# Forming half of w_out's operands beside the first stage, moving the second gate's vector into the feed-forward, and setting the gates' steps later

## The chip, the cores and the metric

The kernel runs on one core of a Trainium2 chip, written in Bass with tile pools: the engines are TensorE (PE), VectorE (DVE), ScalarE (ACT), GpSimd (POOL) and SyncE (SP), which issues nearly all DMAs. Each engine works through its own instructions in order and waits on semaphores for the others. The metric is the device time of one execution in microseconds (us), the median of several runs. A profile is of one further execution.

## The reference

One layer of a hybrid encoder on a sequence of 2048 rows and 1024 columns, in f32: a modulated norm, one input projection that feeds both banded attention (8 heads, 2 key heads) and a bidirectional mLSTM (4 heads, chunks of 128), an output projection, then a SwiGLU feed-forward, and a last norm.

```python
def hybrid_layer(x, c, w_mod, b_mod, ...):
    mod = jax.nn.silu(c) @ w_mod + b_mod
    shift1, scale1, gate1, shift2, scale2, gate2 = split(mod, 6)
    hmix = rms_norm(x, g_norm1) * (1.0 + scale1) + shift1
    proj = hmix @ w_in
    q_a, k_a, v_a, q_m, k_m, v_m, o_m, gates = split(proj, IN_SPLITS)
    att = rms_norm(banded_attention(q_a, k_a, v_a, sink), g_attn_out)
    q_m, k_m = split(silu(centred_dwconv(concat([q_m, k_m]), conv_w, conv_b)), 2)
    i_f, f_f, i_b, f_b = split(gates + b_gates, 4)
    h_m = sigmoid(o_m) * rms_norm(mlstm(fwd) + mlstm(bwd), g_mlstm_out)
    x = x + gate1 * (concat([att, h_m]) @ w_out)
    hff = rms_norm(x, g_norm2) * (1.0 + scale2) + shift2
    gte, up = split(hff @ w_ffn_in, 2)
    return x + gate2 * ((silu(gte) * up) @ w_ffn_out)
```

Two parts matter here: the six vectors of `mod` (rows 0 to 5 of a 1024 x 6144 product; row 2 is gate1, rows 3 and 4 are the feed-forward's shift and scale, row 5 is gate2), and `gate1 * (... @ w_out)`, where the kernel multiplies gate1 into w_out's columns ahead of the product.

## The kernel before

A product in f32 is made of three fast matmuls: each operand is split into a high and a low part (`whi`, `wlo`; ScalarE copies the high part in the fast type, VectorE or GpSimd subtracts), and high x high, high x low and low x high are added in PSUM. TensorE does nearly nothing else, and its order is written out by hand; the other engines' order follows from where the code puts their steps between TensorE's.

**First stage, to about 181 us.** The rows of x are normed, turned and split, and 16 tiles of 128 rows (`tt` 0 to 15) go through the natural projections: `nat_mm` (48 matmuls to a tile, into `pa` and `pv`) gives the values of both attentions, stored in `vst_d` and `vaug_d`, and the gates' pre-activations `gn`. Between the tiles `mod_row(m)` (L359 to L395) forms the vectors of the modulation that are needed later, in two halves of 512 columns: four loads of `wmod`, eight multiply-adds on VectorE into `macc`, a split into `macch` and `maccl`, and a pair of matmuls with ones (`modrow`, L381 and L382). For rows 3 and 4, ScalarE then copies the result to `mrow` (L388), and VectorE turns it into columns (L391). For rows 2 and 5, the gates, VectorE adds the bias (`brow`) and it is stored in `gate_d`. `vecs` gives a half a tile from tile 8 on; before that, row 2 is formed.

**The conv's weights.** `proj_cols` and `cols_steps` (L241 on) load 128 columns of w_in into `wraw`, which has one buffer; `whi` is copied by ScalarE (L251), and four pieces of `wlo` are subtracted by GpSimd (L254). The first such weight, `w_first`, is formed ahead of tile 12; the next, called the second weight below, is loaded when the window begins.

**The window, from 181 to about 245 us.** TensorE runs conv tiles (`gps` L498; 24 matmuls each, eight values of k by three products). Every single matmul is a pull: the generators `gates()` and `w_out_ops()` are given the count of pulls, and go on when it has reached the number that they yielded. Where `gates()` yields 36, its next matmuls (`rps` L871) are issued behind the 36th pull. The gates' chain goes: transposes of `gn`; two copies on ScalarE (L842, L843); exp and log, scans and row sums on VectorE (L845 to L867); `rps`; eight scans `mn` (L881) and the row steps up to `rw` (L888); `cps` (L892); the exponentials; the last transposes. A conv tile writes into one of the `gps` banks of PSUM; ScalarE's copy `cacc` (L525) and VectorE's two side steps (L512, L513) empty it. `w_out_ops()` multiplies w_out's rows by gate1 (`gb`) and forms sums and differences (`ts`) for the products' operands, all on GpSimd, and stores them in `wo_d`. It has eight items: two halves of the columns (`c_`) by four blocks of rows (`k`).

**Later stages.** mLSTM heads 0 to 3 to 573 us, each with a loop backward over the chunks (`cc` from 15 to 0) and one forward; `prep` forms the mask `ng` of a chunk (GpSimd L629, then ScalarE L635) for the forward loop. Attention to 790, the out-projection to 1000, the feed-forward's first product (`fp`) in pairs to 2005, its second (`fo`) to the end. `norm2` forms the feed-forward's input in steps between the pairs.

Of the kernel before, what the change touches and what calls it, by code (L numbers as in the profile page):

```python
# [11 lines left out]
F32 = mybir.dt.float32  # L12
# [24 lines left out]
def hybrid_layer_kernel(  # L37
# [106 lines left out]

    xs, s2s = ExitStack(), ExitStack()
    hp = ctx.enter_context(tc.tile_pool(name="big", bufs=1, side="left"))
# [131 lines left out]
    with tc.tile_pool(name="sw", bufs=2, side="right", reuse_waits="tile") as sw:  # L278
# [80 lines left out]
        def mod_row(m):  # L359

            for z in range(2):
                acc = sw.tile([P, 512], F32, tag="macc", name="macc", bufs=1)
                if m in (2, 5):
                    br = (s1 if m == 2 else wp).tile([1, 512], F32, tag="mrow" if m == 2 else "oth", name="brow", bufs=1)
                    sp.dma_start(br, b_mod[:, m * D + z * 512:m * D + (z + 1) * 512])
                for k in range(0, KT, 2):
                    w = (hp if "b" in wrow[0] else sw if "m" in wrow[0] else wp).tile([P, 2, 512], F32, tag=wrow[0], name="wmod", bufs=1)
                    wrow.rotate(-1)
                    sp.dma_start(w, w_mod[k * P:(k + 2) * P, m * D + z * 512:m * D + (z + 1) * 512]
                                 .rearrange("(k p) c -> p k c", p=P))  # L370
                    for i in range(2):
                        if k + i == 0:
                            dve.tensor_scalar(acc, w[:, 0, :], sc_col[:, 0:1], None, MUL)
                        else:
                            dve.scalar_tensor_tensor(acc, w[:, i, :], sc_col[:, k + i:k + i + 1], acc, MUL, ADD)
# [5 lines left out]
                pe.matmul(ps, ones_r, hi, start=True, stop=False)  # L381
                pe.matmul(ps, ones_r, lo, start=False, stop=True)  # L382
                if m in (2, 5):
                    dve.tensor_tensor(br, ps[:1, :], br, ADD)
                    sp.dma_start(gate_d[m // 5:m // 5 + 1, z * 512:(z + 1) * 512], br)
                    continue
                row = sw.tile([P, 512], F32, tag="macch", name="mrow", bufs=1)
                act.activation(row, ps, AF.Copy)  # L388
                for k in range(4):
                    rk = row[:, k * P:(k + 1) * P]  # L390
                    dve.tensor_tensor_reduce(out=rk, in0=rk, in1=ident, op0=MUL, op1=ADD, scale=1.0, scalar=0.0,  # L391
                                             accum_out=mod[:, m, 4 * z + k:4 * z + k + 1])
            if m not in (2, 5):
                o = O_BM + m * KT
                dve.tensor_tensor(mod[:, m, :], mod[:, m, :], cols[:, o:o + KT], ADD)  # L395

        def nat_mm(n, i, pa, pv, ks):
# [46 lines left out]
        for n in range(NB):  # L444
# [5 lines left out]
            if n == 1:  # L450
# [4 lines left out]
                dve.tensor_scalar(gml, cols[:, O_GM:O_GM + HM], 0.5, None, MUL)  # L455
            if n + 1 == NB:
                w_first = proj_cols(C_KM)
            for i in range(4):
                tt = 4 * n + i
                if tt < 3:  # L460
                    pa, pv = ops[i]
                else:
                    pa, pv = bank("g", "pa"), bank("a", "pv")
# [4 lines left out]
                if tt == 8:  # L468
# [126 lines left out]
    def mlstm(h, nb, nf, last):  # L595
# [45 lines left out]
        for cc in list(range(NT - 1, 0, -1)) + [0, 0, 0]:  # L641
# [6 lines left out]
            if cc in (6, 4, 2):  # L648
                bcs[3 - cc // 2] = load_bc(3 - cc // 2)
            if cc:  # L650
                todo.append((cc, *k_chunk(blk[n][0][:, i * P:(i + 1) * P], blk[n][1][:, i, :], 1, cc)))
                pull(nb - nb // 2)
            if len(todo) > 2 or (todo and not cc):
# [7 lines left out]
                pull(nb // 2)  # L661
        prep(0)
        prep(1)
        decays(0)
# [169 lines left out]
    def gates():  # L834
# [9 lines left out]
        e, u, l, t2 = gt("ge"), gt("gu"), gt("gl"), gt("gt2")  # L844
        dve.scalar_tensor_tensor(e, fg, -1.0, fg, MUL, MIN)  # L845
        act.activation(e, e, AF.Exp)
        dve.tensor_scalar(u, e, 1.0, None, ADD)
# [3 lines left out]
        dve.tensor_tensor(t2, t2, u, MUL)  # L851
        b, r, cm, zr = gt("gb"), gt("grr"), gt("gcm"), gt("gz")
        dve.memset(zr, 0.0)
        rw = s2.tile([1, 3, P], F32, name="rw", bufs=1)
        dve.memset(rw, 0.0)
        dve.tensor_tensor(l, t2, l, SUB)
# [8 lines left out]
        for sl, j in ((lo_, 127), (hi_, 0)):  # L865
            dve.tensor_copy(st[sl, 0:1], b[sl, j:j + 1])
            dve.tensor_tensor(st[sl, 1:2], b[sl, j:j + 1], cm[sl, j:j + 1], ADD)  # L867
        yield 36
        ps = bank("c", "rps")
# [34 lines left out]
        dve.tensor_scalar(ux, ux, -1.0, None, MUL)  # L904
        yield 90
        for d, sl in ((0, lo_), (1, hi_)):
# [25 lines left out]
    def w_out_ops():  # L932

        at_ = [(c_, k) for c_ in range(2) for k in range(4)]
        ready, gb = deque([w_out_load(*at_[0])]), [w_out_gate(0)]
# [3 lines left out]
        for n, (c_, k) in enumerate(at_):  # L939
            at = 16 + 26 * n + 10 * (n > 3)  # L940
            cs = slice(c_ * 256, (c_ + 1) * 256)
# [16 lines left out]
            yield at + 19  # L958
            for u, t in ((0, bx[:, 0]), (1, by[:, 0]), (5, by[:, 1])):
                sp.dma_start(wo_d[u, k][:, cs], t)  # L960
            out_ = [(wo_d[2:4, k, :, cs].rearrange("u p c -> p u c"), ta), (wo_d[4, k][:, cs], tb[:, 0]), (wo_d[6, k][:, cs], tb[:, 1])]
        yield at + 34
# [610 lines left out]
    with tc.tile_pool(name="ff", bufs=1, side="right", reuse_waits="tile") as ff:  # L1573
# [87 lines left out]
        pools["ff"] = ff  # L1661
        pools["xp"] = xp
        norms = deque([norm2(1, 0, "bd", 4), norm2(1, 1, "bd", 1)])
        JO = [m * KH + j for j in range(KH) for m in range(2)]
        units = [(0, j) for j in JO] + [(1, j) for j in reversed(JO)]
        wseq = deque(JO[2:] + JO[-2::-1])
        raw, more_w = (*raws[0], load_a22(KH)), None
        for n, (hh, j) in enumerate(units[:-1]):
# [7 lines left out]
            def beside(u):  # L1676
# [287 lines left out]
```

## Time and profile before

| what | us |
|---|---|
| median of 3 runs | 2267.78 (2266.62 to 2268.79) |
| the profiled execution, its own time | 2268.64 |
| its span | 2266.8 |
| granted TensorE clock, mean over the span | 0.995 of full speed |
| TensorE busy | 2223.8 |

The span is the time from the first to the last event of the profiled execution. The page gives each engine's busy time and a chain of waits: the work that ended last, followed back. The timeline has one row for each instruction or group of them: start, duration, engine, line, operation, output and inputs, and in brackets the engine's idle time before it and what ended it. A window row has the stretch, its length, the busy time and the number of instructions of PE, PE's weight loads, DVE, ACT and POOL, the granted clock, the share of time in which the DMA engines are busy, and GB/s.

### The profile page before, as it was taken

What the parts mean: (1) busy time and instruction counts of PE and PEld (TensorE: products, weight loads), DVE (VectorE), ACT (ScalarE), POOL (GpSimd) and SP (SyncE); (2) the same over time, 40 slices, a digit from 0 to 9 for tenths busy, and PEclk for the clock granted to TensorE, in tenths of its full rate; (3) what the DMA queues carried; (4) which work ended last, traced back from release to release, by engine and by line L of the source; (5) the groups of instructions that cost most, each with busy time, mean ns of one, the idle gap of its engine ahead of it and who ended that gap; (6) DMA issues with size and microseconds to landing.
All of it is one profiled execution on the core that took longest, in us unless ns stands there. A gap on an engine that the chain in (4) does not pass through costs nothing.

```text
span 2266.8 us, 32424 instructions
## 1 busy us (share of the span) xinstructions
PE 2223.8 (98%) x10822; PEld 1858.7 (82%) x10822; DVE 1611.1 (71%) x2944; ACT 1060.3 (47%) x2206; POOL 1040.6 (46%) x914
## 2 busy tenths in 40 slices
PE   6999999999999999999999999999999999999998
PEld 4997888888888878888888888888888888878887
DVE  6787577656688877886767786766666665785694
ACT  5433565654677746354444444433333333233452
POOL 1006635334344333436666674457566654692020
PEclk9999999999999999999999999999999999999999
DMA  8476755586666576764343454433333374542462
GB/s 329 161 244 209 246 166 168 182 240 180 205 186 183 174 243 207 268 235 150 108 149 112 158 181 164 157 98 111 98 112 98 112 260 142 176 142 94 144 217 93
DMA packets 352811, 391.28 MB, mean 173 GB/s; under 512 B 21260, under 2 KB 251004, under 8 KB 352644
## 3 DMA queue, kind: packets, MB, share of 16 engines
q1 hardware_dynamic: 352420, 389.18, 52.6%
q8 instruction: 85, 1.39, 0.2%
q14 instruction: 82, 0.67, 0.1%
q10 hardware_dynamic: 224, 0.04, 0.0%
HBM read 269.95 MB, written 119.19 MB: 172 GB/s over the span
## 4 chain that ended last, share of the span: by engine, by line
PE 88%; DVE 4%; ACT 3%; DMA 2%; issue 1%; POOL 1%; SPq 0%; ACTq 0%; POOLq 0%; DVEq 0%
PE gps L498 14%; PE fp L56 12%; PE fp L57 12%; PE fp L58 12%; PE fo L56 6%; PE fo L58 6%; PE fo L57 6%; PE ops L56 2%; PE ops L58 2%; PE ops L57 2%; PE kvp L622 1%; PE num L709 1%; PE num L711 1%; PE atp L805 1%; ACT ap L788 1%
## 5 line engine op out<-in xcount | busy, mean ns | idle before, releaser
L498 PE MATMUL gps<-hT,whi 128*128 128x512 f32 x1088 | 396.5, 419 | 0.3 <-DVE cacc L513 0.3
L56 PE MATMUL fo<-w,ah 128*128 128x512 f32 x616 | 239.9, 389 | 1.0 <-DVE rb L1876 1.0
L58 PE MATMUL fo<-w,al 128*128 128x512 f32 x616 | 239.9, 389 | 0.1
L57 PE MATMUL fo<-w,ah 128*128 128x512 f32 x616 | 239.7, 389 | 0.0
L498 PE MATMUL gps<-hT,wlo 128*128 128x512 f32 x544 | 226.7, 417 | 0.0
L498 PEld LDWEIGHTS gps<-hT,whi 128*128 128x128 f32 x1088 | 200.2, 190 | 24.7 <-DVE cacc L513 0.7
L56 PE MATMUL fp<-T,S 128*128 128x512 f32 x528 | 206.7, 391 | 0.3 <-ACT s L1610 0.3
L57 PE MATMUL fp<-T,S 128*128 128x512 f32 x528 | 205.6, 389 | 0.0
L58 PE MATMUL fp<-T,S 128*128 128x512 f32 x528 | 205.4, 389 | 0.0
L1718 DVE TENSOR_TENSOR al<-al,ah 128x1024 fp32r<-128x1024 f32 x77 | 117.4, 1530 | 108.0 <-ACT ah L1717 108.0
L1717 ACT ACTIVATE ah<-al 128x1024 fp32r<-128x1024 f32 x77 | 81.6, 1060 | 182.8 <-DMA al<-a_d 180.3
L1453 DVE TENSOR_TENSOR S<-sf,S 128x512 fp32r<-128x512 f32 x86 | 129.8, 1547 | 34.4 <-ACT S L1452 34.2
L1453 DVE TENSOR_TENSOR A<-graw,A 128x512 fp32r<-128x512 f32 x86 | 130.8, 1541 | 13.2 <-ACT A L1452 12.8
L58 PE MATMUL fp<-B,A 128*128 128x512 f32 x352 | 136.9, 389 | 0.0
L56 PE MATMUL fp<-B,A 128*128 128x512 f32 x352 | 136.9, 389 | 0.0
L57 PE MATMUL fp<-B,A 128*128 128x512 f32 x352 | 136.9, 389 | 0.0
L56 PEld LDWEIGHTS fo<-w,ah 128*128 128x128 f32 x616 | 115.6, 188 | 25.4 <-DVE rb L1876 1.8
L58 PEld LDWEIGHTS fo<-w,al 128*128 128x128 f32 x616 | 115.6, 188 | 24.7 <-DVE al L1718 0.5
L57 PEld LDWEIGHTS fo<-w,ah 128*128 128x128 f32 x616 | 115.6, 188 | 24.2
L1620 DVE SCALAR_TENSOR_TENSOR g<-t,g 128x512 f32<-128x512 f32 x44 | 41.8, 950 | 131.3 <-ACT t L1619 131.3
L798 POOL TENSOR_SCALAR ap<-ap,adn 128x384 f32<-128x384 f32 (+1 forms) x128 | 73.5, 594 | 125.7 <-PE atp L805 58.6
L1457 POOL TENSOR_TENSOR sf<-A,A22r 128x512 f32<-128x512 f32 x42 | 58.1, 1383 | 145.5 <-DMA A22r<-in_w_ffn_in_dram 118.5
(427 smaller groups left out, 6142.2 us busy)
## 6 DMA issues: line engine op xcount, KB each, us to landing
al<-a_d SPq DMA_DIRECT2D x77, 512.0 KB, 3.8
wmod<-in_w_mod_dram SPq DMA_DIRECT2D x48, 512.0 KB, 7.6
graw<-in_w_ffn_in_dram SPq DMA_DIRECT2D x43, 512.0 KB, 3.9
a_d<-ka SPq DMA_DIRECT2D x66, 256.0 KB, 4.7
bc<-bc_d SPq DMA_DIRECT2D x64, 256.0 KB, 3.7
hop_d<-n SPq DMA_DIRECT2D x56, 256.0 KB, 4.0
a_d<-u SPq DMA_DIRECT2D x55, 256.0 KB, 4.6
mqk<-qk_d SPq DMA_DIRECT2D x44, 256.0 KB, 3.8
```

Source lines behind the costliest of these rows:

```text
L56: pe.matmul(o, lh, rh, start=first, stop=False, skip_group_check=skip)
L57: pe.matmul(o, lh, rl, start=False, stop=False, skip_group_check=skip)
L58: pe.matmul(o, ll, rh, start=False, stop=last, skip_group_check=skip)
L498: pe.matmul(ps, w[i == 2][:, k, :], hT[n](i == 1, k), start=(k == 0 and i == 0), stop=(k == KT - 1 and i == 2))
L622: pe.matmul(kvp[:, :129], kn, vw, start=True, stop=True)
L709: pe.matmul(num[:, d, :129], sc[:, d, :], va_c, start=True, stop=st is None)
L798: pool.tensor_scalar(self.p[g][:, :self.NK], self.p[g][:, :self.NK], dn[:, g:g + 1], 0.0, MUL, ADD)
L1453: dve.tensor_tensor(t[:, 1, :], f, t[:, 0, :].bitcast(F32), SUB)
L1457: add.tensor_tensor(f1, a21, a22, ADD)
L1620: dve.scalar_tensor_tensor(g0, t0, 1.0, g0, ADD, MUL)
L1717: act.activation(ah, al.bitcast(F32), AF.Copy)
L1718: dve.tensor_tensor(al, al.bitcast(F32), ah.bitcast(F32), SUB)
```

## The change

Five edits:

1. `mod_row` no longer forms row 5. A new generator, `gate2()`, forms it in the feed-forward, one step in every unit after the first half of them: eight loads of 128 x 1024, one multiply and seven multiply-adds on VectorE, a split, four matmuls, and the store.
2. A new generator, `w_out_all()`, forms w_out's operands for k = 0 and 1, all columns, beside tiles 8 to 15, with GpSimd; SyncE is put into manual order there (`wxs`), and a pool `wx` holds two more tiles. Rows 3 and 4 of the modulation now take a half in every second tile. `w_first` is formed ahead of tile 14.
3. `w_out_ops()` keeps k = 2 and 3, begins at pull 54 instead of 16, and stores with fewer DMAs.
4. The gates' steps come at pulls 44, 78 and 104 instead of 36, 66 and 90; two memsets are written earlier.
5. `prep(0)` and `prep(1)` stand in the backward loop at `cc` 3 and 1 instead of behind it.

```diff
-                if m in (2, 5):
+                if m == 2:
...
+        def w_out_all():
+            gb = wp.tile([P, 2, 512], F32, tag="wraw", name="gbb", bufs=1)
+            sp.dma_start(gb.rearrange("p m c -> p (m c)"), gate_d[0, :].partition_broadcast(P))
+            for k in range(2):
+                if k:
+                    yield True
+                bx, by = (wp.tile([P, 2, 512], F32, tag=tag, name="wox", bufs=1) for tag in ("w0h", "w0l"))
+                for t, k_ in ((bx, k), (by, k + 4)):
+                    sp.dma_start(t, w_out[k_ * P:(k_ + 1) * P].rearrange("p (m c) -> p m c", m=2))
+                yield True
+                for t in (bx, by):
+                    pool.tensor_tensor(t, t, gb, MUL)
+                ta, tb = (wx.tile([P, 2, 512], F32, tag=n, name=n, bufs=1) for n in ("wta", "wtb"))
+                for t, f, g in (...):
+                    pool.tensor_tensor(t, f, g, SUB)
+                yield True
+                sp.dma_start(wo_d[0, k], bx[:, 0])
+                for u, t in ((slice(1, 6, 4), by), (slice(2, 4), ta), (slice(4, 7, 2), tb)):
+                    sp.dma_start(wo_d[u, k].rearrange("u p c -> p u c"), t)
...
-            if n + 1 == NB:
-                w_first = proj_cols(C_KM)
             for i in range(4):
                 tt = 4 * n + i
+                if tt == NT - 2:
+                    w_first = proj_cols(C_KM)
...
+                    wx = wxs.enter_context(tc.tile_pool(name="wx", bufs=1, side="left", reuse_waits="tile"))
+                    wxs.enter_context(tc.manual_schedule(engines={mybir.EngineType.SP}))
+                    parts = w_out_all()
-                    vecs = chain.from_iterable(mod_row(m) for m in range(3, 6))
+                    vecs = chain.from_iterable(mod_row(m) for m in (3, 4))
...
-                if tt != 9:
+                if tt < 9 or tt % 2 == 0:
                     next(vecs, None)
...
+                if tt >= 8:
+                    next(parts, None)
         deque(vecs, 0)
+        wxs.close()
...
+            if cc in (3, 1):
+                prep(1 - cc // 2)
...
-        prep(0)
-        prep(1)
...
-        yield 36
+        yield 44
...
-        yield 66
+        yield 78
...
-        yield 90
+        yield 104
...
-        at_ = [(c_, k) for c_ in range(2) for k in range(4)]
+        at_ = [(c_, k) for c_ in range(2) for k in range(2, 4)]
...
-            at = 16 + 26 * n + 10 * (n > 3)
+            at = 54 + 26 * n + 10 * (n > 1)
...
+        def gate2():
+            row = lambda n, dt=F32: ff.tile([P, D], dt, tag="xt", name=n, bufs=4)
+            wr, acc, br = [row("wmod") for _ in range(2)], row("macc"), row("brow")
+            sp.dma_start(br[:1, :], b_mod[:, 5 * D:6 * D])
+            def fetch(k):
+                sp.dma_start(wr[k % 2], w_mod[k * P:(k + 1) * P, 5 * D:6 * D])
+            fetch(0)
+            yield True
+            for k in range(KT):
+                if k + 1 < KT:
+                    fetch(k + 1)
+                if k == 0:
+                    dve.tensor_scalar(acc, wr[0], sc_col[:, 0:1], None, MUL)
+                else:
+                    dve.scalar_tensor_tensor(acc, wr[k % 2], sc_col[:, k:k + 1], acc, MUL, ADD)
+                yield True
+            hi, lo = row("macch", F32R), row("maccl", F32R)
+            split(acc, hi, lo)
+            yield True
+            for z in range(2):
+                ps, zs = bank("bd"[z], "modrow"), slice(z * 512, (z + 1) * 512)
+                pe.matmul(ps, ones_r, hi[:, zs], start=True, stop=False)
+                pe.matmul(ps, ones_r, lo[:, zs], start=False, stop=True)
+                dve.tensor_tensor(br[:1, zs], ps[:1, :], br[:1, zs], ADD)
+            yield True
+            sp.dma_start(gate_d[1:2, :], br[:1, :])
...
+                if n > NJ and u == 1:
+                    next(gate, None)
```

What the edits do to the engines' order shows at three places. The first is SyncE at the end of the first stage. `wmod` is a load for a modulation row, `wraw` one of a conv weight, `wox`, `wta` and `wtb` are the new stores of w_out's operands, and `bx` is the first load of the window. Before:

```order
L487 DMA vaug_d<-va 128x516
L369 DMA wmod<-in_w_mod_dram 128x2x512 x4
L486 DMA vst_d<-vs 128x256
L385 DMA gate_d<-brow 1x512
L487 DMA vaug_d<-va 128x516
L247 DMA wraw<-in_w_in_dram 128x8x128
L365 DMA brow<-in_b_mod_dram 1x512
L486 DMA vst_d<-vs 128x256
L487 DMA vaug_d<-va 128x516
L385 DMA gate_d<-brow 1x512
L922 DMA bx<-in_w_out_dram 128x2x256
```

After:

```order
L415 DMA wo_d<-wox 128x512
L417 DMA wo_d<-wox 128x2x512
L417 DMA wo_d<-wta 128x2x512
L417 DMA wo_d<-wtb 128x2x512
L247 DMA wraw<-in_w_in_dram 128x8x128
L369 DMA wmod<-in_w_mod_dram 128x2x512 x4
L511 DMA vst_d<-vs 128x256
L512 DMA vaug_d<-va 128x516
L247 DMA wraw<-in_w_in_dram 128x8x128
L511 DMA vst_d<-vs 128x256
L512 DMA vaug_d<-va 128x516
L950 DMA bx<-in_w_out_dram 128x2x256
```

Before, the one `wraw` here is the second weight's, and the first weight's stood some twenty rows earlier. Now both stand here, the first behind the stores of w_out's operands and ahead of the last four loads of `wmod`, the second three rows behind those.

The second place is ScalarE at the same time, from tile 15's copies (`va`) to the window's first conv copy (`cacc`). Before:

```order
L481 ACTIVATE va<-pa 128x128
L251 ACTIVATE whi<-wraw 128x1024
L141 ACTIVATE macch<-macc 128x512
L482 ACTIVATE va<-pv 128x3x128
L842 ACTIVATE gates<-gps 128x128
L843 ACTIVATE gates<-gps 128x128
L846 ACTIVATE gates<-gates 128x128
```

After:

```order
L507 ACTIVATE va<-pv 128x3x128
L251 ACTIVATE whi<-wraw 128x1024
L503 ACTIVATE vs<-pa 128x2x64
L141 ACTIVATE macch<-macc 128x512
L506 ACTIVATE va<-pa 128x128
L251 ACTIVATE whi<-wraw 128x1024
L388 ACTIVATE mrow<-modrow 128x512
L870 ACTIVATE gates<-gps 128x128
L871 ACTIVATE gates<-gps 128x128
L878 ACTIVATE gates<-gates 128x128
```

The first `whi` of the changed order is the first weight's and stands behind a `va` copy of `pv`, which is tile 15's; the second `whi` is the second weight's. Between it and the gates' copies stands `mrow` of row 4's second half, where before the last row was row 5, which has no `mrow`.

The third place is GpSimd at the end of head 0, where `hst` ends the head's sums and `ng` is the mask of a later chunk. Before:

```order
L730 TENSOR_TENSOR hst<-hst,mry 128x512
L254 TENSOR_TENSOR wlo<-wraw,whi 128x256
L629 TENSOR_TENSOR ng<-bc,maskb 128x256 x2
L684 TENSOR_TENSOR qs<-mqk,bc 128x256
L629 TENSOR_TENSOR ng<-bc,maskb 128x256
L254 TENSOR_TENSOR wlo<-wraw,whi 128x256 x2
```

After:

```order
L758 TENSOR_TENSOR hst<-hst,mry 128x512
L657 TENSOR_TENSOR ng<-bc,maskb 128x256 x2
L254 TENSOR_TENSOR wlo<-wraw,whi 128x256
L712 TENSOR_TENSOR qs<-mqk,bc 128x256
L657 TENSOR_TENSOR ng<-bc,maskb 128x256
L254 TENSOR_TENSOR wlo<-wraw,whi 128x256 x2
```

The two `ng` of `prep(0)` and `prep(1)` have gone ahead of the weight's first `wlo`.

More of the change, by code (lines that the diff above doesn't have):

```diff
@@ L362, in mod_row @@
                 acc = sw.tile([P, 512], F32, tag="macc", name="macc", bufs=1)
-                if m in (2, 5):
-                    br = (s1 if m == 2 else wp).tile([1, 512], F32, tag="mrow" if m == 2 else "oth", name="brow", bufs=1)
+                if m == 2:
+                    br = s1.tile([1, 512], F32, tag="mrow", name="brow", bufs=1)
                     sp.dma_start(br, b_mod[:, m * D + z * 512:m * D + (z + 1) * 512])
@@ L845, in gates @@
         dve.scalar_tensor_tensor(e, fg, -1.0, fg, MUL, MIN)
+        b, r, cm, zr = gt("gb"), gt("grr"), gt("gcm"), gt("gz")
+        dve.memset(zr, 0.0)
+        rw = s2.tile([1, 3, P], F32, name="rw", bufs=1)
+        dve.memset(rw, 0.0)
         act.activation(e, e, AF.Exp)
@@ L958, in w_out_ops @@
             yield at + 19
[L959 to L961 removed]
+            sp.dma_start(wo_d[0, k][:, cs], bx[:, 0])
+            sp.dma_start(wo_d[1:6:4, k, :, cs].rearrange("u p c -> p u c"), by)
+            out_ = [(wo_d[u, k, :, cs].rearrange("u p c -> p u c"), t) for u, t in ((slice(2, 4), ta), (slice(4, 7, 2), tb))]
         yield at + 34
@@ L1662, in hybrid_layer_kernel @@
         pools["xp"] = xp
+        def gate2():
[24 more added lines that the diff above has]
+            sp.dma_start(gate_d[1:2, :], br[:1, :])
         norms = deque([norm2(1, 0, "bd", 4), norm2(1, 1, "bd", 1)])
+        gate = gate2()
         JO = [m * KH + j for j in range(KH) for m in range(2)]
```

14 lines of the change are left out of this document (6 added, 8 removed).

## Prediction

> **What bounds the kernel now.** I read the page's busy times first, then the chain of waits, then the windows and the timeline around 175 to 205 us, where most of the edits sit.
>
> ```profile
> span 2266.8 us, 32424 instructions
> PE 2223.8 (98%) x10822; PEld 1858.7 (82%) x10822; DVE 1611.1 (71%) x2944; ACT 1060.3 (47%) x2206; POOL 1040.6 (46%) x914
> PE 88%; DVE 4%; ACT 3%; DMA 2%; issue 1%; POOL 1%; SPq 0%; ACTq 0%; POOLq 0%; DVEq 0%
> ```
>
> TensorE is busy for 2223.8 of 2266.8 us, so it idles for 43 us in all. Work on the other engines is free as long as TensorE does not wait for it. An edit counts only where it adds TensorE work, removes or makes a TensorE wait, or changes the granted clock. The windows show the clock (the column before the DMA share) and, last, the DMA rate in GB/s:
>
> ```profile
> 35.00:40.00 5.00, 5.00 (x36) 5.00 (x36) 4.82 (x7) 0.00 (x0) 0.49 (x2) 1.00 1.04 412
> 160.00:165.00 5.00, 4.78 (x32) 4.25 (x31) 4.13 (x14) 1.93 (x4) 0.00 (x0) 1.00 0.87 293
> 180.00:185.00 5.00, 4.25 (x12) 3.17 (x13) 2.61 (x6) 3.09 (x7) 3.26 (x4) 0.70 0.25 87
> 1500.00:2000.00 500.00, 499.96 (x2206) 413.64 (x2206) 333.88 (x297) 176.49 (x289) 313.17 (x194) 1.00 0.42 140
> ```
>
> The feed-forward (last row) leaves TensorE 0.04 us of idle time in 500, while VectorE is busy for 67%. The end of the first stage (third row) has waits and a clock of 0.70. The timeline of TensorE shows why:
>
> ```profile
> 122.93 0.37 PE L56 MATMUL pa<-wnh,hT 128*128 128x272 f32 x1
> 130.23 0.29 PE L56 MATMUL pa<-wnh,hT 128*128 128x272 f32 x1
> 137.45 0.40 PE L381 MATMUL modrow<-macch,ones_r 128*128 128x512 f32 x1
> 178.44 0.33 PE L58 MATMUL pv<-wnh,hT 128*128 128x384 f32 x1
> 180.42 0.50 PE L381 MATMUL modrow<-macch,ones_r 128*128 128x512 f32 x1 [1.65 <-ACT macch L141]
> 181.25 0.50 PE L382 MATMUL modrow<-maccl,ones_r 128*128 128x512 f32 x1 [0.33 <-DVE maccl L142]
> 181.72 0.93 PE L498 MATMUL gps<-hT,whi 128*128 128x512 f32 x2
> 185.44 0.63 PE L498 MATMUL gps<-hT,whi 128*128 128x512 f32 x2
> 188.20 0.61 PE L498 MATMUL gps<-hT,whi 128*128 128x512 f32 x2
> 188.88 0.61 PE L498 MATMUL gps<-hT,whi 128*128 128x512 f32 x2
> 191.69 0.60 PE L871 MATMUL rps<-ident,gates 128*1 128x128 f32 x4
> 199.28 0.60 PE L892 MATMUL cps<-ones_r,rw 1*128 1x1 f32 x4
> 200.18 0.74 PE L498 MATMUL gps<-hT,whi 128*128 128x512 f32 x2
> 202.12 0.74 PE L498 MATMUL gps<-hT,whi 128*128 128x512 f32 x2 [0.27 <-DVE cacc L513]
> ```
>
> Tile 15 ends at 178.6. TensorE then waits 1.65 + 0.33 us for the last row of the modulation. Three conv matmuls take 188.88 - 188.20 = 0.68 us, 0.227 each; the nine from 181.72 to 185.44 take 3.72 instead of 2.04, so the low clock costs 1.7 us. The gates' first result comes at 191.69 (`rps`, after 36 pulls), just in time, and the fourth conv tile starts at 202.12.
>
> **First stage, end of tile 15.** A tile of 48 matmuls takes 130.23 - 122.93 = 7.30 us, or 137.45 - 130.23 = 7.22. From tile 9 on, the changed order has three `modrow` pairs of 0.46 us between tiles. Tile 15 ends at 122.93 + 7.30 + 6 x 7.22 + 3 x 0.46 = 174.9, some 3.7 us earlier. That gain lasts only if what follows is ready.
>
> **The second conv weight is late.** These rows carry the sum:
>
> ```profile
> 178.79 1.06 ACT L251 ACTIVATE whi<-wraw 128x1024 fp32r<-128x1024 f32 x1 [0.32 <-DMA wraw<-in_w_in_dram]
> 180.27 0.47 ACT L482 ACTIVATE va<-pv 128x384 f32<-128x384 f32 x1
> 179.92 3.34 POOL L254 TENSOR_TENSOR wlo<-wraw,whi 128x256 fp32r<-128x256 f32 x4 [12.45 <-ACT whi L251]
> 173.04 5.57 DMA wraw<-in_w_in_dram
> DMA to landing us min/median/max: 4.2/5.6/6.1
> 154.30 0.60 ACT L388 ACTIVATE mrow<-modrow 128x512 f32<-128x512 f32 x1 [0.83 <-PE modrow L382]
> 139.62 0.29 DVE L391 CUSTOM_DVE_ANT_0 mrow<-mrow,ident 128x128 f32<-128x128 f32 x1
> 140.46 0.74 DVE L375 SCALAR_TENSOR_TENSOR macc<-wmod,sc_col,macc 128x512 f32<-128x512 f32 x1
> 182.40 0.27 DVE L845 SCALAR_TENSOR_TENSOR gates<-gates 128x128 f32<-128x128 f32 x1
> 185.92 0.17 DVE L853 MEMSET gates<- 128x128 f32 x1
> 190.46 1.17 DVE L867 TENSOR_TENSOR gates<-gates 64x1 f32<-64x1 f32 x1
> ```
>
> `wraw` has one buffer. In the changed order the first weight's split on ScalarE stands behind tile 15's copy, and the second weight's load needs that split done by ScalarE and GpSimd. Ahead of the gates' copies, in ScalarE's order, stands the second weight's own split: whatever delays that load delays the gates. Step by step:
>
> - tile 15 ends 174.9, copy 0.5, so 175.4;
> - first split, from `whi`'s start to the last `wlo` 179.92 + 3.34 - 178.79 = 4.47, so 179.9; load issued at 180.0;
> - landing 5.57 (bounds 4.2 and 6.1), so 185.6; `whi` 1.06, so 186.7; `mrow` 0.60, so 187.3;
> - VectorE's four column sums, 140.46 - 139.62 = 0.84, and the bias, an estimate of 1.1 together, so 188.4;
> - the gates' chain 191.63 - 182.40 = 9.23, less about 0.35 for two memsets that now lie in a wait (185.92 and the one behind it), 8.9: `rps` at 197.3.
>
> TensorE would be at pull 44 at 191 to 193: the first `whi` ends at 176.5, and the last row's split, its pair and the gates' transposes take it to about 179 (an estimate from the waits of 180.42 and 181.25); 44 x 0.227 = 10.0 and 1.7 of low clock make 191, and 2 more if the last `wmod` lands late. The eight extra pulls (1.8 us) do not cover the rest to 197.3.
>
> **The next wait, at pull 72.** From `rps` to the fourth conv tile, before, took 202.12 - 191.69 = 10.43 us. It is a chain: eight scans and the row steps on VectorE, the exponential on ScalarE, then a conv copy behind it on ScalarE and the sides on VectorE, which free the PSUM bank that the fourth tile writes. It was covered by 36 matmuls and `cps`. Now `rps` comes 28 pulls ahead of that tile, 28 x 0.227 = 6.4 us plus its own 0.5, and the chain is as long. TensorE waits 3 us or more there even if the gates are on time; here the tile starts at 197.3 + 10.4 = 207.7 instead of 202.12: **+5.6** (4.2 to 6.1, by the bounds of the landing). `cps` (200.18 - 199.28 = **+0.9**) was ahead of that point and is now behind it.
>
> After waits the clock falls, as in 180 to 185. The rows nearest to a wait of 10.4 - 6.9 = 3.5 us:
>
> ```profile
> 830.00:834.00 4.00, 0.94 (x3) 0.48 (x3) 4.00 (x5) 2.14 (x4) 2.75 (x2) 1.00 0.18 53
> 834.00:838.00 4.00, 2.75 (x8) 2.38 (x9) 1.56 (x3) 0.97 (x2) 3.92 (x5) 0.50 0.00 0
> 343.14 0.49 PE L622 MATMUL kvp<-vw,kn 128*128 128x129 f32 x2 [1.22 <-ACT vw L617]
> 341.94 0.69 ACT L635 ACTIVATE ng<-ng,rT 128x128 f32<-128x128 f32 x2 [1.54 <-POOL ng L629]
> 341.16 1.42 POOL L629 TENSOR_TENSOR ng<-bc,maskb 128x256 f32<-128x256 f32 x2
> ```
>
> With 3 of 4 us idle the clock is 0.50 in the next 4 us. I take the same 1.7 us as at 181.72 (**+1.7**; bounds 0, as after the 1.22 us at 343.14, and 1.7). [...]
>
> **Moved heads' preparation.** At 343.14 TensorE waited 1.22 us: ScalarE's `ng` waited for GpSimd's, which stood behind a weight's `wlo`, and the copy for `kvp` stood behind it. In the changed order both `ng` come ahead of that `wlo`: **-1.1** (0 to -1.2). The two `ng` of each later head move into loop steps in the same way; I cost them at nothing.
>
> **Second gate's vector.** It leaves the first stage (counted in tile 15's end) and gives the feed-forward four matmuls of 128x512, 4 x 0.227 = **+0.9**. There TensorE has no idle time to take them. Its VectorE steps:
>
> ```profile
> L1718 DVE TENSOR_TENSOR al<-al,ah 128x1024 fp32r<-128x1024 f32 x77 | 117.4, 1530 | 108.0 <-ACT ah L1717 108.0
> ```
>
> Nine operations of about 1.5 us each, one to a unit, fit into VectorE's free third, and its 4 MB into a DMA share of 0.42: zero. Without that cover each would delay a unit by up to 1.5 us, 14 us at most; I see no reason for it.
>
> **w_out beside the stage, and its other half.** Its loads and stores go by SyncE and its arithmetic by GpSimd, idle there (0.00 busy in 160 to 165). The price is DMA traffic, in rival B. In the window half the items are left, later; TensorE waited for none of them before, so they bring nothing.
>
> **Sum.** +5.6 + 0.9 + 1.7 - 1.1 + 0.9 = +8.0 on the profiled execution of 2268.64 us (span 2266.8 and 1.84 around it), 2276.6. That execution is 0.9 above the median of 2267.78, so **2275.8** is predicted for the median.
>
> **Rivals.**
>
> *B, the DMA queue saturates.*
>
> ```profile
> wmod<-in_w_mod_dram SPq DMA_DIRECT2D x48, 512.0 KB, 7.6
> ```
>
> From tile 8 to the last row's landing I count 17.8 MB by the tiles' sizes: 8.4 of `wmod` (16 loads), 2.6 of loads and 3.7 of stores for w_out, 2.3 of `vst` and `vaug`, 0.8 more. In the 56.5 us to 180 that needs 315 GB/s. The windows show 293 at a share of 0.87, and 412 at most. At 293 the traffic ends at 123.5 + 17800/293 = 184.3, and the second weight lands at about 190 instead of 185.6: 4.4 more, **2280**. Against it: at 35 us the engines moved 412.
>
> *C, the second weight is not late* (its landing by 181.5, because the first split runs earlier than I read it). Then only the wait at pull 72 is left: pull 44 at 192.8, fourth tile 10.4 later at 203.2, so +1.1 + 0.9 + 1.7 - 1.1 + 0.9 = +3.5, **2271.3**. For it speaks only that a load can land in 4.2 us.
>
> *D, faster.* With fewer rows left, the last modulation row is ready when tile 15 ends, so the waits of 1.65 + 0.33 and the 1.7 of low clock go, the gates start at 175.4, and no chain of theirs is waited for. Pull 44 comes at 174.9 + 0.5 (pair) + 0.3 (transposes) + 44 x 0.227 = 185.7, the fourth tile 10.4 later at 196.1, 6.0 before its time: -6.0 + 0.9 + 0.9 - 1.1 = -5.3 with the clock kept, **2262.5**. It decides if ScalarE has the second weight by about 175; the single `wraw` buffer speaks against it.
>
> **How the numbers follow.** The forecast has a chance of 0.50, with a range of its own of 2272 (landing 4.2, no clock loss) to 2278; B 0.17, C 0.18, D 0.13, the rest 0.02. From C's low end and part of D to above B: 2267 to 2281. A change of 0.2% (4.5 us) is about what can be told from none. D gives faster 0.13; C, ending within 4.5 us, and the low edge of the forecast give 0.23 for the same; forecast and B give 0.64.
>
> **What would show it.** In the changed trace: tile 15 ends near 175; `whi` of the second weight on ScalarE starts near 185.6, released by its DMA; `rps` waits on VectorE until about 197; the fourth conv tile waits about 3 us for `cacc`; no 1.2 us wait at head 1's start; the feed-forward's pair time unchanged but for 0.9. If `rps` does not wait, the reading of ScalarE's order is wrong; if `macch` of the last row waits for `wmod` beyond 184, B holds.

## The result, and the profile after

| | before | changed |
|---|---|---|
| median of 6 runs, us | 2267.82 | 2283.6 |
| lowest to highest | 2266.62 to 2268.79 | 2281.91 to 2288.52 |
| ratio, 95% interval | | 1.0074, 1.0063 to 1.0085 |
| span of the profiled execution | 2266.8 | 2280.9 |

The change costs 15.8 us, twice the forecast of 8.0, and ends above the forecast's range. First, where. The view of the tile `kvp` gives the first and the last start of head 0's to head 3's matmuls; before and after:

```profile
L622 PE MATMUL kvp<-vw,kn x240: 271/273/378, 245.3 to 559.6; 128*128 128x129 f32 x120
```

```profile
L650 PE MATMUL kvp<-vw,kn x240: 271/273/378, 261.0 to 573.8; 128*128 128x129 f32 x120
```

Head 0 starts 15.7 us later; the last chunk of head 3 comes only 14.2 later, so the heads gain 1.5. The first `fp` matmul moves by 13.9 (996.0 to 1009.9), the first `fo` by 14.9 (1837.7 to 1852.6; so the feed-forward's first product ends at 1837.7 before, not at 2005): that product loses 1.0. So the loss lies ahead of 261 us, and the start of head 0 is the mark by which the experiments are compared below. TensorE's timeline of the changed kernel there (start, duration, idle time before and its releaser):

```profile
172.00 0.79 PE L381 MATMUL modrow<-macch,ones_r 128*128 128x512 f32 x1 [4.19 <-ACT macch L141]
182.64 0.33 PE L58 MATMUL pv<-wnh,hT 128*128 128x384 f32 x1
190.93 0.80 PE L381 MATMUL modrow<-macch,ones_r 128*128 128x512 f32 x1 [7.96 <-ACT macch L141]
208.19 0.38 PE L899 MATMUL rps<-ident,gates 128*1 128x128 f32 x2 [4.03 <-DVE gates L894]
```

Tile 15 ends at 182.8, not at 174.9. TensorE waits 4.19 us for the first half of row 4, 7.96 for the second, and 4.03 for the gates. VectorE, GpSimd and SyncE show why the halves are late:

```profile
160.03 1.00 DVE L373 TENSOR_SCALAR macc<-wmod,sc_col 128x512 f32<-128x512 f32 x1 [4.53 <-DMA wmod<-in_w_mod_dram]
161.07 10.21 DVE L375 SCALAR_TENSOR_TENSOR macc<-wmod,sc_col,macc 128x512 f32<-128x512 f32 x7
171.20 0.28 DVE L504 TENSOR_TENSOR vs<-pa,vs 128x128 fp32r<-128x128 f32 x1
182.78 0.49 DVE L373 TENSOR_SCALAR macc<-wmod,sc_col 128x512 f32<-128x512 f32 x1 [7.38 <-DMA wmod<-in_w_mod_dram]
183.31 6.91 DVE L375 SCALAR_TENSOR_TENSOR macc<-wmod,sc_col,macc 128x512 f32<-128x512 f32 x7
```

```profile
160.71 2.58 POOL L409 TENSOR_TENSOR wox<-wox,gbb 128x1024 f32<-128x1024 f32 x1
163.38 1.62 POOL L413 TENSOR_TENSOR wtb<-wox 128x512 f32<-128x512 f32 x1
164.95 1.74 POOL L413 TENSOR_TENSOR wta<-wox,wta 128x512 f32<-128x512 f32 x1
166.77 1.61 POOL L413 TENSOR_TENSOR wtb<-wox,wta 128x512 f32<-128x512 f32 x1
```

```profile
153.66 2.48 SPq L369 DMA_DIRECT2D wmod<-in_w_mod_dram  x4
...
171.51 0.32 SPq L511 DMA_DIRECT2D vst_d<-vs  x1
...
176.54 3.20 SPq L369 DMA_DIRECT2D wmod<-in_w_mod_dram  x4
...
188.91 0.38 SPq L247 DMA_DIRECT2D wraw<-in_w_in_dram  x1
```

Seven multiply-adds take 10.21 us, 1.46 each on average, where one took 0.76 before. GpSimd's w_out steps run until 168.4. Narrower windows show single ones of the seven, the first, the second and then the fifth and sixth together:

```profile
161.07 2.77 DVE L375 SCALAR_TENSOR_TENSOR macc<-wmod,sc_col,macc 128x512 f32<-128x512 f32 x1
163.88 1.66 DVE L375 SCALAR_TENSOR_TENSOR macc<-wmod,sc_col,macc 128x512 f32<-128x512 f32 x1
168.96 1.54 DVE L375 SCALAR_TENSOR_TENSOR macc<-wmod,sc_col,macc 128x512 f32<-128x512 f32 x2
```

The four beside GpSimd take 1.6 to 2.8 us, each ending some 0.55 us behind a step of GpSimd; the three behind its last step take about 0.76 again. The store `vst_d` on SyncE waits for VectorE's `vs`, which stands behind these seven; the next `wmod` loads stand behind that store and w_out's stores, and go at 176.54. VectorE's first product on them starts at 182.78, released by their DMA; then seven more multiply-adds, and the row is there at 190.9. The second weight's load waits for the first's split, as forecast (ScalarE):

```profile
192.44 1.06 ACT L251 ACTIVATE whi<-wraw 128x1024 fp32r<-128x1024 f32 x1 [1.40 <-DMA wraw<-in_w_in_dram]
193.41 0.58 ACT L388 ACTIVATE mrow<-modrow 128x512 f32<-128x512 f32 x1
193.88 0.27 ACT L870 ACTIVATE gates<-gps 128x128 f32<-128x128 f32 x1
```

### The profile page after: what moved, and what is told of

Read it like the earlier page. It is cut to its first block, busy times and chain, and to the rows that moved or that the text cites. A ratio compares the mean times of both kernels' runs of the same rounds, so it can differ in the third digit from the quotient of the medians.

```text
span 2280.9 us, 32341 instructions
## 1 busy us (share of the span) xinstructions
PE 2227.3 (98%) x10822; PEld 1863.1 (82%) x10822; DVE 1623.2 (71%) x2935; ACT 1059.3 (46%) x2205; POOL 1041.9 (46%) x902
## 4 chain that ended last, share of the span: by engine, by line
PE 85%; DVE 6%; ACT 3%; DMA 2%; issue 2%; POOL 1%; SPq 0%; ACTq 0%; POOLq 0%; DVEq 0%
PE gps L526 14%; PE fp L56 12%; PE fp L57 12%; PE fp L58 12%; PE fo L58 5%; PE fo L57 5%; PE fo L56 5%; PE ops L56 2%; PE ops L58 2%; PE ops L57 2%; PE kvp L650 1%; PE num L737 1%; PE num L739 1%; ACT ap L816 1%; PE atp L833 1%
```

## The experiments

The table gives each run's median, its ratio to the kernel before with the interval, and the start of head 0 in its profile (before 245.3, changed 261.0).

| run | median, us | ratio | head 0, us |
|---|---|---|---|
| e1_sp_auto | 2281.42 | 1.0061 (1.0045 to 1.0078) | 258.3 |
| e2_no_arith | 2275.46 | 1.0037 (1.0024 to 1.0050) | 253.4 |
| e3_no_early | 2268.14 | 1.0003 (0.9994 to 1.0013) | 244.6 |
| e8_pool_only | 2279.34 | 1.0050 (1.0033 to 1.0066) | 257.3 |
| e6_no_early_y36 | 2264.90 | 0.9993 (0.9985 to 1.0002) | 242.5 |
| e9_every_tile | 2282.18 | 1.0070 (1.0057 to 1.0083) | 260.8 |
| e10_every_no_arith | 2273.73 | 1.0035 (1.0023 to 1.0046) | 253.4 |
| e12_pool_memset | 2270.54 | 1.0016 (1.0007 to 1.0025) | 248.3 |
| e14_prefetch | 2283.35 | 1.0069 (1.0054 to 1.0085) | 265.2 |
| e14b_prefetch_no_arith2 | 2275.46 | 1.0034 (1.0021 to 1.0047) | 253.4 |
| e16_second_later | 2279.30 | 1.0050 (1.0035 to 1.0065) | 255.8 |
| e18_all_three | 2269.04 | 1.0003 (0.9994 to 1.0013) | 248.8 |
| e21_no_wout_dma | 2282.05 | 1.0071 (1.0057 to 1.0085) | 244.6 |
| e22_no_wout_second_later | 2279.49 | 1.0059 (1.0045 to 1.0072) | 241.8 |
| e7_y36 | 2285.27 | 1.0087 (1.0072 to 1.0102) | 261.4 |
| e17_best | 2264.07 | 0.9986 (0.9977 to 0.9995) | 240.7 |
| e25_quarter_bytes | 2285.78 | 1.0081 (1.0054 to 1.0109) | 249.8 |

**SyncE's order.**

```diff
-                    wxs.enter_context(tc.manual_schedule(engines={mybir.EngineType.SP}))
```

> The changed kernel with SyncE's order left to the scheduler beside tiles 8 to 15 instead of set by hand. Theory P (GpSimd's two-operand steps of w_out stretch VectorE's row sums, so the modulation rows come late): the same GpSimd work runs, so within 4 us of the changed kernel's 2283.6. Rival S (SyncE's order by hand keeps the rows' loads behind the stores): the loads start earlier and the time falls below 2278. Rival F (the forecast: the second conv weight is late): within 4 us of 2283.6, because that load still waits for the first weight's split.

2281.4, 2.7 us earlier at head 0: the scheduler's order puts the last row's loads behind the same store too (`vst_d` at 171.48, the loads at 174.50), and SyncE's order by hand is not the loss.

**GpSimd's arithmetic, taken away and added alone.** Without it:

```diff
-                for t in (bx, by):
-                    pool.tensor_tensor(t, t, gb, MUL)
...
-                    pool.tensor_tensor(t, f, g, SUB)
+                for t in (ta, tb):
+                    act.activation(t, gb, AF.Copy)
```

> The changed kernel without GpSimd's six multiplications and subtractions for each of w_out's blocks k = 0 and 1 beside the first stage (two ScalarE copies stand in their place, so w_out's operands for these blocks are not formed); all loads and stores stay. Theory P: each multiply-add on VectorE there takes 0.76 us throughout, the waits of 4.2 and 8.0 us for the last two rows shrink to 3 us or less, and the time is 2268 to 2275. Rival S and a full DMA queue: the loads come as late as before, 2280 to 2285. Rival F: the wait for rps stays and the waits for the rows too, 2280 or more.

Added to the kernel before, with nothing else but two ScalarE copies that fill the scratch tiles:

```diff
+                if tt in (9, 12):
+                    for t in (ta, tb):
+                        pool.tensor_tensor(t, t, ta, MUL)
+                    for t, f, g in (...):
+                        pool.tensor_tensor(t, f, g, SUB)
```

> The kernel before the change with nothing but the same twelve GpSimd steps (four of 128x1024, eight of 128x512) added on two scratch tiles beside tiles 9 and 12; no DMA is added and nothing uses the result. Theory P: VectorE's multiply-adds beside them take 1.2 to 1.7 us instead of 0.76, the last row comes 5 to 10 us later, 2273 to 2279. Rivals S, F and a full DMA queue: GpSimd was idle there, so no change, 2266 to 2269.

Twelve steps on an engine that was nearly idle (busy for 5.4 us from 123 to 181 before), whose results nobody reads, cost 12.0 us at head 0, a little more than expected. The groups of VectorE's multiply-adds from 125 to 200 us (busy time, mean ns of one) before, in e8_pool_only and in e2_no_arith:

```profile
L375 DVE SCALAR_TENSOR_TENSOR macc<-wmod,sc_col,macc 128x512 f32<-128x512 f32 x42 | 32.1, 763 | 0.9
```

```profile
L375 DVE SCALAR_TENSOR_TENSOR macc<-wmod,sc_col,macc 128x512 f32<-128x512 f32 x42 | 40.5, 964 | 0.9
```

```profile
L375 DVE SCALAR_TENSOR_TENSOR macc<-wmod,sc_col,macc 128x512 f32<-128x512 f32 x28 | 22.5, 805 | 4.2 <-DMA wmod<-in_w_mod_dram 3.1
```

In e8_pool_only, six of them beside GpSimd take 11.83 us, and TensorE waits 6.38 at the first row:

```profile
129.80 11.83 DVE L375 SCALAR_TENSOR_TENSOR macc<-wmod,sc_col,macc 128x512 f32<-128x512 f32 x6
```

```profile
144.01 0.79 PE L381 MATMUL modrow<-macch,ones_r 128*128 128x512 f32 x1 [6.38 <-ACT macch L141]
```

Without the steps (e2_no_arith) head 0 starts 7.6 us earlier than in the changed kernel. The upper end of what was expected is just missed, because a wait of 7.85 us for the last row stays:

```profile
182.43 0.79 PE L381 MATMUL modrow<-macch,ones_r 128*128 128x512 f32 x1 [7.85 <-ACT macch L141]
```

In the changed kernel a multiply-add took 1.6 to 2.8 us beside GpSimd's steps and about 0.76 behind them. Those steps read two operands each and write one. Whether steps that only write hold VectorE up as well was tried with memsets in place of the twelve:

```diff
-                        pool.tensor_tensor(t, t, ta, MUL)
+                        pool.memset(t, 1.0)
```

> The kernel before the change with twelve GpSimd memsets of the same sizes in the places of the twelve two-operand steps of e8_pool_only: GpSimd writes and reads nothing. If VectorE's two-operand instructions are held up by GpSimd's reads only: VectorE's multiply-adds keep 0.76 us, 2265 to 2269. If any GpSimd work beside them holds them up: 2272 or more.

2270.5, between the two cases. A memset takes 0.5 to 0.95 us where the steps of e8_pool_only took 1.4 to 2.7, so all twelve had run by 133.6 us. They fell beside VectorE's first product of a row:

```profile
128.57 3.64 DVE L373 TENSOR_SCALAR macc<-wmod,sc_col 128x512 f32<-128x512 f32 x1 [1.21 <-DMA wmod<-in_w_mod_dram]
```

That one took 3.64 us instead of 0.49, beside memsets that ran back to back: they held up this product, which has one tensor input, and its 3.15 us more are near the 3.0 by which head 0 starts later. Only two multiply-adds fell beside memsets:

```profile
131.87 0.80 POOL L495 MEMSET wtb<- 128x512 f32 x1
132.61 0.52 POOL L495 MEMSET wta<- 128x512 f32 x1
133.07 0.52 POOL L495 MEMSET wtb<- 128x512 f32 x1
132.24 1.54 DVE L375 SCALAR_TENSOR_TENSOR macc<-wmod,sc_col,macc 128x512 f32<-128x512 f32 x2
```

Both kept their 0.76 us, 1.54 for the two, but two are few: why the product was held and they were not is not shown.

**Without w_out beside the stage.**

```diff
-                    parts = w_out_all()
...
-        at_ = [(c_, k) for c_ in range(2) for k in range(2, 4)]
+        at_ = [(c_, k) for c_ in range(2) for k in range(4)]
...
-                if tt == NT - 2:
-                    w_first = proj_cols(C_KM)
+            if n + 1 == NB:
+                w_first = proj_cols(C_KM)
```

> The changed kernel without w_out's operands beside the first stage: all eight items of w_out in the window as before, the first conv weight ahead of tile 12, SyncE's order left to the scheduler, rows 3 and 4 a half a tile; the second gate in the feed-forward, the later gates' steps and the moved preparation stay. Theory P and rival S: no wait at the end of the first stage, the window starts 3 to 4 us earlier than before the change, 2262 to 2267. If the gates' later pulls or the second gate's place cost several us by themselves, over 2272.

2268.1, 1.1 above the range expected: all of the loss is gone, but nothing is won. The end of the stage has no wait; the fourth conv tile has one, as forecast for the changed kernel. Eight scans and TensorE of e3_no_early:

```profile
189.53 3.54 DVE L881 TENSOR_TENSOR_SCAN mn<-sr 1x16 f32<-1x16 f32 x8 [2.06 <-ACT sr L873]
```

```profile
199.23 0.79 PE L498 MATMUL gps<-hT,whi 128*128 128x512 f32 x1 [3.53 <-DVE cacc L513]
```

The same scans before, beside GpSimd's items, and in the changed kernel, where GpSimd was through with its first items:

```profile
193.11 3.98 DVE L881 TENSOR_TENSOR_SCAN mn<-sr 1x16 f32<-1x16 f32 x8
210.05 0.77 DVE L909 TENSOR_TENSOR_SCAN mn<-sr 1x16 f32<-1x16 f32 x8
```

With the pulls back:

```diff
-        yield 44
+        yield 36
...
-        yield 78
+        yield 66
...
-        yield 104
+        yield 90
```

> The version without w_out's operands beside the first stage (e3_no_early) with the gates' steps back at pulls 36, 66 and 90. Theory G (the pulls of 44 and 78 leave too few matmuls over the chain from rps to the fourth conv tile while GpSimd slows it): the 3.5 us wait for cacc of e3_no_early goes to 1 us or less, 2262 to 2266. Rival: the gates are late anyway and the wait only moves to rps: 2266 to 2269.

2264.9 and no wait at that tile: the later pulls cost about 2 us at head 0 (244.6 to 242.5) where GpSimd slows the scans (3.54 us). The same edit on the changed kernel:

> The changed kernel with the gates' steps back at pulls 36, 66 and 90. rps waits for its chain there either way, and GpSimd is through with w_out's first items when the scans run, so nothing is queued up to gain: 2282 to 2286. If the later pulls cost by themselves, as e3_no_early against e6_no_early_y36: 2279 to 2281.

2285.3, nothing gained: `rps` waits 6.33 us at pull 36 instead of 4.03 at pull 44.

**The rows' places.** In the changed kernel, and in e2_no_arith:

```diff
-                if tt < 9 or tt % 2 == 0:
+                if tt != 9:
```

> The changed kernel with rows 3 and 4 taking a half in every tile from 8 on but 9, as before the change, instead of every second tile. Theory P with its second half (GpSimd's steps and the late loads of rows that come only every second tile share the loss about equally): the wait of 8 us for the last row goes, some is paid at the earlier rows, 2273 to 2280. If GpSimd alone makes the loss: 2281 to 2286. If the rows' places alone make it: 2268 to 2272.

> Both: the rows in every tile, and GpSimd's steps beside the stage left out as in e2_no_arith (w_out's operands for k = 0 and 1 are not formed). Theory P with its second half: no wait of over 1 us for a row; what is left is the second conv weight behind tile 15 and the gates behind it, rps at about 197, 2267 to 2273. If the second weight costs nothing: 2266 or less. If rows and steps are not all of it: over 2274.

Head 0 starts at 260.8 and 253.4, as without the edit, so the spacing is not the loss. The one long wait behind tile 15 becomes waits of 6.73, 2.39 and 3.67 us between the tiles (e9_every_tile), and of 2.71, 2.60 and 1.15 us in e10_every_no_arith, where none over 1 us was expected. Next, each half's loads issued ahead of the stores between, with and without the arithmetic:

```diff
                 split(acc, hi, lo)
+                if (m, z) in ((3, 0), (3, 1), (4, 0)):
+                    load_rows(m + z, 1 - z)
                 yield True
```

> The changed kernel with the four loads of each next half row issued as soon as the last multiply-adds of the half before are written, so ahead of the stores of the tiles between. Theory L (beside GpSimd's steps, the loss comes from the loads of a row that stand on SyncE behind a store that waits for VectorE): the wait of 8 us for the last row shrinks by 4 us or more, 2276 to 2280. If the loads' place costs nothing: 2282 to 2286.

> The same with GpSimd's steps beside the stage left out as in e2_no_arith (w_out's operands for k = 0 and 1 are not formed). Theory L: the wait of 7.9 us for the last row in e2_no_arith goes to 1 us or less, tile 15 ends near 176 and the gates wait for the second conv weight only: 2266 to 2271. If the loads' place costs nothing: 2274 to 2277, as e2_no_arith.

That theory fell: the medians stay, and head 0 starts at 265.2 (in a run 3.3 us above its median) and 253.4. The waits for rows go, but VectorE now takes multiply-adds of the next row, and the column sums, ahead of the step `vs` that helps to empty PSUM, and TensorE waits for the copy `va` behind it (e14b_prefetch_no_arith2):

```profile
140.60 0.28 DVE L512 TENSOR_TENSOR vs<-pa,vs 128x128 fp32r<-128x128 f32 x1
141.34 0.39 PE L56 MATMUL pa<-wnh,hT 128*128 128x272 f32 x1 [3.71 <-ACT va L514]
```

**The second weight's split behind the gates' copies.**

```diff
-    w_second = proj_cols(C_QM)
+    g_second = cols_steps(C_QM)
+    next(g_second)
...
+        if i in (45, 50, 55, 60):
+            ready[0] = next(g_second)
```

> The changed kernel with the second conv weight's split put at pulls 45 to 60 instead of ahead of the window, so behind the gates' copies on ScalarE. Rival F, as far as it is left (the second weight holds up the gates): the gates' copies start about 1.3 us earlier, their chain is not stretched by that weight's steps on GpSimd, rps comes 3 to 5 us earlier: 2278 to 2281. If it costs nothing: 2282 to 2286.

> The three together: loads ahead, GpSimd's steps left out (w_out's operands for k = 0 and 1 are not formed), the second weight's split behind the gates' copies. If GpSimd's steps, the loads' place and the second weight are the whole loss: TensorE waits less than 1 us from 150 us to the fourth conv tile, 2261 to 2267. If something else is left: 2269 or more.

In the changed kernel it is worth 5.2 us at head 0 (261.0 to 255.8), as expected. The three edits together leave 3.5 us over the kernel before (248.8 to 245.3), with waits of 3.7 us for `va` and 2.8 for `gn`: something was left, and w_out's DMAs were the next thing to take away.

**w_out's DMAs.**

```diff
-                    parts = w_out_all()
+                    parts = iter(())
...
+            for k in range(2):
+                for u in range(7):
+                    sp.dma_start(wo_d[u, k], w_out[k * P:(k + 1) * P, 0:512])
```

> The changed kernel with nothing of w_out's blocks k = 0 and 1 beside the first stage, neither loads nor arithmetic nor stores (fourteen copies in device memory in head 1 stand in for the stored operands, whose values are wrong); rows 3 and 4 still in every second tile, the first weight ahead of tile 14. Against e2_no_arith (2275.5, wait of 7.9 us for the last row): if w_out's DMAs make the rows' loads late, that wait shrinks by 4 us or more and the time is 2268 to 2271; if it is the rows' places and SyncE's order alone, 2274 to 2277.

> The same as e21_no_wout_dma with the second weight's split behind the gates' copies, as in e16_second_later. If the second weight is the rest of the loss: 3 to 5 us under e21_no_wout_dma, 2263 to 2268; if not, within 1.5 us of it.

The whole times miss, because a load of head 1 stands behind the fourteen copies on SyncE: head 0 starts at 244.6 in e21_no_wout_dma, but head 3's last chunk comes at 572.0, later than the 559.6 before.

```profile
339.57 0.45 PE L640 MATMUL ktp<-ident,mqk 128*128 128x128 f32 x1 [12.67 <-DMA mqk<-qk_d]
```

Up to head 0 the answer is plain: with the DMAs gone too (and the four ScalarE copies that stood in for the arithmetic), 8.8 us more are won (253.4 to 244.6), and the second weight is worth 2.8 of what is left (241.8). A window over tiles 8 to 15 in e2_no_arith and in e21_no_wout_dma:

```profile
123.00:180.00 57.00, 51.58 (x340) 51.00 (x338) 31.05 (x74) 15.42 (x32) 4.36 (x10) 0.98 0.93 321
```

```profile
123.00:180.00 57.00, 54.86 (x350) 53.36 (x349) 34.38 (x81) 14.26 (x34) 6.49 (x13) 0.97 0.70 227
```

The DMA engines' share falls from 0.93 to 0.70. Is it the bytes, or the places in SyncE's queue? The places kept, a quarter of the bytes:

```diff
-                    sp.dma_start(t, w_out[...])
+                    sp.dma_start(t[:, :, :128], w_out[...][:, :, :128])
```

> e2_no_arith (no GpSimd steps of w_out beside the stage) with every load and store of w_out's blocks there kept in its place on SyncE but cut to the first 128 of 512 columns, a quarter of the bytes; copies in device memory in head 1 fill the rest, so only the times up to head 0 are compared: the first kvp matmul of head 0 starts at 253.4 in e2_no_arith and at 244.6 in e21_no_wout_dma. If the bytes make the rows' loads late, it starts at 244 to 247; if their place in SyncE's queue does, at 251 to 254. The whole time is 2278 to 2290 either way, for the copies.

249.8 lies between: 3.6 us by the bytes cut, 5.2 by places and what bytes are left. Both take part; which has how much stays open. The traces show where each acts. The last row's loads and VectorE's first product on them in e2_no_arith, then in e21_no_wout_dma:

```profile
167.83 3.07 SPq L369 DMA_DIRECT2D wmod<-in_w_mod_dram  x4
174.15 0.48 DVE L373 TENSOR_SCALAR macc<-wmod,sc_col 128x512 f32<-128x512 f32 x1 [4.83 <-DMA wmod<-in_w_mod_dram]
```

```profile
161.34 3.23 SPq L369 DMA_DIRECT2D wmod<-in_w_mod_dram  x4
167.77 0.80 DVE L373 TENSOR_SCALAR macc<-wmod,sc_col 128x512 f32<-128x512 f32 x1 [4.08 <-DMA wmod<-in_w_mod_dram]
```

From issue to product it is 6.3 us and 6.4: this row does not land more slowly, it is issued 6.5 us later, behind a store that waits for VectorE (162.99 instead of 158.51) and behind w_out's four stores. The row before it, loaded right behind w_out's loads, does land more slowly: 6.1 us (149.60 to 155.74) instead of 4.7 (147.46 to 152.14).

**A version that beats both.** e6_no_early_y36, with rows 3 and 4 in every second tile:

```diff
-                if tt != 9:
+                if tt < 9 or tt % 2 == 0:
```

> e6_no_early_y36 with rows 3 and 4 taking a half in every second tile. The waits of 2.4 and 0.2 us for rows in e6_no_early_y36 go, since VectorE has two tiles for each: 2261 to 2265. If the loads come as late as in e2_no_arith, the last row is waited for: 2266 to 2272.

2264.1: 0.14% under the kernel before (0.05 to 0.23), and by the two ratios some 20 us under the changed one. TensorE has no wait in 123 to 180:

```profile
123.00:180.00 57.00, 57.00 (x368) 55.80 (x367) 36.01 (x94) 17.23 (x38) 7.47 (x14) 1.00 0.68 215
```

So the rows' places cost nothing where nothing else disturbs them. What is left there is a wait for the gates:

```profile
187.01 0.81 PE L871 MATMUL rps<-ident,gates 128*1 128x128 f32 x4 [3.10 <-DVE gates L866]
```

## Why the prediction was wrong

The step that failed is this one: w_out's "arithmetic by GpSimd, idle there (0.00 busy in 160 to 165). The price is DMA traffic". The arithmetic was costed at nothing, and the traffic was put off to a rival. The runs show 7.6 us for the arithmetic (261.0 to 253.4; 12.0 when added alone) and 8.8 for the DMAs (253.4 to 244.6), 16.4 together; the rest of the change ahead of head 0 gains 0.7 against the kernel before. The parts hold for this order of taking them away: the DMAs were neither added alone nor taken away with the arithmetic left in. The trace of before had a sign of it: the last `gates` row of L867 took 1.17 us there beside GpSimd, and 0.15 in e3_no_early without.

- *Tile 15's end, 174.9.* Measured 182.8, for the same reason: the sum had no wait for a row. There was one of 4.19 us, and 2.3 us of low clock behind it (24 `pa` matmuls took 5.29 us from 173.32, at a granted clock of 0.52, and 3.00 from 153.24, at 1.00). Without w_out's steps and DMAs (e21_no_wout_dma) the tile did end at 174.8.
- *The second weight is late.* The order was read rightly, and its split is released by its DMA ahead of the gates' copies. The load was issued at 188.9 instead of 180.0 and took 3.5 us to `whi`, not 5.57. Its worth, 5.2 us in the changed kernel, is near the 5.6 forecast, but it came on top of a stage that was already late.
- *Column sums and bias, 1.1 us, and the gates' chain, 8.9 us.* The first took 3.1 (from `mrow`'s end at 193.99 to L873 at 197.04), beside GpSimd's split of the second weight; from L873 to `rps` at 208.19 it took 11.2, beside GpSimd's steps of the window. Both sizes came from rows with less of GpSimd beside them.
- *The wait at pull 72.* It did not come in the changed kernel: there the eight scans took 0.77 us, not the 3.98 of before, and the step L541 that frees the bank ended 6.1 us behind `rps`, not 10.4. The 10.4 us taken from before held GpSimd's share. In e3_no_early, where the scans took 3.54, the wait came with 3.53 us.
- *The clock.* It fell in and behind the waits, as at 830 us before (0.50 from 834 to 838), and at more than the one place of the sum:

```profile
185.00:190.00 5.00, 0.00 (x0) 0.00 (x0) 4.86 (x5) 0.28 (x1) 3.88 (x4) 0.52 0.44 164
190.00:195.00 5.00, 4.07 (x10) 2.97 (x11) 2.18 (x7) 2.67 (x6) 1.42 (x2) 0.50 0.87 251
```

- *The moved preparation, -1.1, and the second gate, +0.9.* The wait of 1.22 us is gone in the changed kernel, and the heads gain 1.5; the feed-forward's first product loses 1.0. Neither size is settled: in e3_no_early, with the same move, a wait of 1.0 us stands there, and e8_pool_only and e12_pool_memset, without the second gate's matmuls, lose 0.4 and 0.7 in that product against the kernel before.
- *Rival B.* Right that the DMA traffic counts, too small at 4.4 us, and not by its mechanism alone: it took a full queue at 293 GB/s, but a share of 0.93 moves 321 (e2_no_arith), and the last row's first load was there at 182.78, ahead of the 184 named as its sign. What hurts most is the row whose loads stand behind the stores: TensorE waited 7.96 us for it in the changed kernel and 7.85 in e2_no_arith.

## What to carry to other kernels

An idle engine was not free room here: twelve steps put on GpSimd cost 12.0 us at head 0 (e8_pool_only), paid for by the VectorE instructions beside them, so price such work by what those take in the trace while GpSimd runs, and by who waits for them. A chain's length taken from one trace held only for the neighbours that it had there: 10.4 us behind `rps` before, 6.1 in the changed kernel. When loads and stores are added beside a stage, look at what stands behind them in the same queue and at what the next load waits for, not only at the bytes.

## What the runs showed of the hardware

Beside GpSimd's two-operand steps a 128x512 multiply-add on VectorE took two to four times its time (1.6 to 2.8 us in the changed kernel, 1.97 on average in e8_pool_only, 0.76 without), and eight scans of 1x16 took 3.98 us in the kernel before, and 0.77 in the changed one behind GpSimd's steps. GpSimd memsets, back to back, held one VectorE product with a single tensor input for 3.64 us instead of 0.49 (e12_pool_memset), and left two multiply-adds at 0.76 (same run). Fourteen copies of 256 KB within device memory, issued in head 1, made TensorE wait 12.67 us for a load behind them and moved head 3's last chunk by 13.1 us against head 0's first (from 314.3 us between them before to 327.4 in e21_no_wout_dma).
